# A hybrid decoder step on one core: mask product over 512 columns, small tiles that share areas, a 54th buffer, and a deeper look-ahead in one stretch

## The chip, the cores and the metric

The kernel is one program for one NeuronCore of a Trainium2 chip. The metric is the device time of one execution in microseconds (us). The engines have names here as in the profile: PE (TensorE, matrix products), DVE (VectorE), ACT (ScalarE), POOL (GpSimd) and SP (SyncE, which only issues DMAs). Each engine works through its own list of instructions in order; an instruction that waits holds up all that stand behind it on its engine. PE writes to PSUM, and all the rest works in SBUF or moves between SBUF and device memory by DMA.

## The reference

Two residual layers over 1024 prompt tokens and 8 single new tokens, 2048 channels, all in float32:

```
layer A:  u, gate = x @ w_in_a
          d = trailing mean of u over 2, 4, 8 or 16 tokens (by channel group) - u
          d = (d by group @ w_grp) * scale
          x = LayerNorm(alpha * x + (d * silu(gate)) @ w_out_a)
shared:   k, v = x @ w_kv            # 4 heads of 64; the first 16 dims of k rotated
layer B:  q, gate = x @ w_in_b       # 32 heads of 64; q rotated
          s = q.k / 8 over the last 128 keys; p = exp(s - m) / (sum + exp(sink - m))
          x = LayerNorm(alpha * x + ((p @ v) * silu(gate)) @ w_out_b)
outputs:  x of both token sets, the last 15 pooled rows, the last 128 keys and values
```

In layer B a query at position i of a block of 128 sees the keys 0 to i of its own block and the keys i+1 to 127 of the block before it: 128 keys exactly, split at the diagonal.

## The kernel before, in words

Tokens are worked on in two chunks, c = 0 with 512 and c = 1 with 512 + 8. Channels lie on the partitions. Phases follow each other: "ai" and "ao" (layer A's input and output projection), "bi" and "bo" (layer B's), each for chunk 0 and then chunk 1.

**Products.** The large projections take float32 operands apart: a high part (`cast_to`, ACT, L488) and a low part (`prep_to`, DVE, L503), and three matmuls stand for one (high by high, high by low, low by high; L658 to L660). All but two phase parts use Strassen's scheme: of a pair of output tiles, seven products of 24 matmuls each, whose weight sums are made by DVE (L346 in `first_pair`, L293) and written back for the second chunk. The two plain parts (start of ai0, first half of bi0) use units of 48 matmuls over 512 columns (L686 to L688).

**Look-ahead.** Before each product `begin` runs `load_to(e + a)`, `prep_to(e + d)` and `cast_to(e + b)`: weight loads run `a` products ahead, casts `b`, low parts `d`. The three numbers are 7, 4, 3. From the last pair of queries in bi1 until the 23rd product of bo0 they are 6, 3, 2 (`self.ahead`, set in `queries`). In bi1, `begin` also falls back to 6, 3, 2 when fewer than four buffers are free. This order of the source is kept on PE, DVE and ACT (`in_order`); SP and POOL are ordered by the scheduler of the framework.

**Buffers.** Nearly everything in SBUF lives in one pool (`Mem`) of 53 buffers of 128 x 1040 float32, handed out whole (`full`) or as halves (`half`). `full` takes the buffer given up longest ago. A buffer that was given up by an instruction that has not run yet is no error: whoever writes to it first waits for that instruction. How early side work starts (normalisation, weight sums, activation loads) depends on how many buffers are free.

**Attention** (`attend`, one call for two heads and one chunk, 32 calls). PE's scores (L1760) put 256 keys per block into PSUM: 128 of the block before, 128 of its own. ACT copies the earlier keys to SBUF (L1778), DVE overwrites those at or before the query by the own block's scores where an int32 mask says so (L1782, `copy_predicated`), finds the largest (L1786), ACT takes the exponentials (L1797) and scales by the sums (`norm`, L1810, eight pieces of 128 columns). PE turns the eight 128 x 128 pieces (L1814), ACT copies them (L1823), and DVE makes a second, masked copy (L1824: 1024 columns, times +1, 0 or -1). The values are then two kinds of products (L1848): one half of the keys times all queries as if it belonged wholly to one block, and a correction, the masked copy times the difference of the two blocks' values (`Vd`). Of each 128 queries the correction reads only 64 columns.

Queries come from products; `q_done` swaps rows by four DMAs on SP (`partner`, L1616), and DVE rotates (L1624 twice, then the sum L1731). The first scores of a pair need L1731. The gate's half of layer B's projection, the decode tokens (`decode`) and the output products run between.

**Small tiles.** Constants (`cst`: identity, mask, a matrix of 1/2048, pooling factors), parameters (`prm`), the int32 mask, negated sinks, the carried pooling rows, and three small tiles of the decode tokens (of which two exist twice) have areas of their own.

## Time and profile before

| | us |
|---|---|
| median of 3 runs | 2360.77 (2357.7 to 2366.27) |
| the profiled execution | 2356.38 |
| its span, first to last instruction | 2354.6 |
| PE busy | 2297.3 |
| DVE busy | 1925.9 |
| ACT busy | 1343.1 |

How to read the profile. A row of a timeline has the start (us), the length (us), the engine, the source line, the operation, what it writes and reads, and in brackets how long the engine had been idle and what ended that. A row of the table of waits has the waiting engine, tile and line, what ended the wait, the sum in us, how often, and the longest. In a table of groups the last fields are the busy time, the mean length in ns and the idle time before. A stretch has its bounds and length and then the busy time of each engine with its count of instructions; "PEclk" is the granted share of TensorE's clock. SPq is SP's queue: the length there is the issue.

### The profile page before, as it was taken

Reading aid. Unit: us, or ns where it says so; the run is one execution under the profiler, and the core shown is the slowest. Engines: PE = TensorE matmul, PEld = TensorE weight load, DVE = VectorE, ACT = ScalarE, POOL = GpSimd, SP = SyncE. Lnnn points to the kernel's source line nnn. Section 1 sums busy time; section 2 is a strip of 40 time slices with the busy share of each in tenths; the row PEclk is TensorE's granted clock in tenths of the full one; section 3 lists DMA queues with packets and bytes.
Section 4 is the critical chain, followed back from the end, with each engine's and each line's share of the span. In section 5 each row is a group of like instructions: output and inputs, shape, how many; then the busy total and the mean of one; then the engine's idle time right before and its main releaser. Section 6 shows DMA issues by size and latency. Waiting matters only on the chain. (4 is left out here: it accounts for less than half of the span.)

```text
span 2354.6 us, 49710 instructions
## 1 busy us (share of the span) xinstructions
PE 2297.3 (98%) x19960; PEld 2200.9 (93%) x19960; DVE 1925.9 (82%) x2421; ACT 1343.1 (57%) x2429; POOL 205.5 (9%) x411
## 2 busy tenths in 40 slices
PE   8999999999999999999999899999999999999997
PEld 6899999999999999998788799999999999999997
DVE  8787998776878878978987788887777768888887
ACT  4444446544546547554465566685666678546556
POOL 0111110001000000000111111100000000000000
PEclk9999999999999999999999999999999999999999
DMA  8668789989889989999786766688777768799785
GB/s 293 211 246 303 271 299 346 332 292 319 289 289 339 327 280 333 328 388 327 272 310 220 248 219 239 224 310 270 237 249 245 230 201 305 239 342 372 260 300 199
DMA packets 250919, 665.18 MB, mean 283 GB/s; under 512 B 25632, under 2 KB 106432, under 8 KB 250688
## 3 DMA queue, kind: packets, MB, share of 16 engines
q1 hardware_dynamic: 205216, 496.94, 63.0%
q0 software_dynamic: 45472, 165.07, 18.1%
q8 instruction: 156, 2.56, 0.4%
q14 instruction: 75, 0.61, 0.1%
HBM read 466.81 MB, written 185.59 MB: 277 GB/s over the span
## 5 line engine op out<-in xcount | busy, mean ns | idle before, releaser
L658 PE MATMUL pD<-m,m 128*128 128x260 f32 (+1 forms) x4752 | 1346.0, 283 | 8.1 <-ACT pD L599 4.4
L660 PE MATMUL pD<-m,m 128*128 128x260 f32 (+1 forms) x4752 | 1339.1, 282 | 4.4 <-DVE m L503 4.4
L659 PE MATMUL pD<-m,m 128*128 128x260 f32 (+1 forms) x4752 | 1338.8, 282 | 0.0
L658 PEld LDWEIGHTS pD<-m,m 128*128 128x128 f32 x4752 | 894.5, 188 | 13.7 <-ACT pD L599 5.5
L660 PEld LDWEIGHTS pD<-m,m 128*128 128x128 f32 x4752 | 895.2, 188 | 5.5 <-DVE m L503 5.5
L503 DVE TENSOR_TENSOR m<-m,m 128x1024 fp32r<-128x1024 f32 x674 | 814.5, 1219 | 100.1 <-ACT m L488 60.6
L659 PEld LDWEIGHTS pD<-m,m 128*128 128x128 f32 x4752 | 894.9, 188 | 0.5
L488 ACT CAST m<-m 128x1024 fp32r<-128x1024 f32 x674 | 702.7, 1049 | 324.7 <-DVE m L346 85.1
L686 PE MATMUL pD<-m,m 128*128 128x512 f32 x448 | 179.7, 401 | 8.0 <-ACT m L769 8.0
L687 PE MATMUL pD<-m,m 128*128 128x512 f32 x448 | 177.9, 397 | 1.0 <-DVE m L778 1.0
L688 PE MATMUL pD<-m,m 128*128 128x512 f32 x448 | 177.5, 396 | 0.0
L778 DVE TENSOR_TENSOR m<-m,m 128x1024 fp32r<-128x1024 f32 (+1 forms) x120 | 147.0, 1226 | 6.4 <-ACT m L769 4.7
L769 ACT CAST m<-m 128x1024 fp32r<-128x1024 f32 (+1 forms) x120 | 125.9, 1053 | 17.7 <-PE pD L687 5.2
L631 ACT COPY m<-pD 128x260 f32<-128x260 f32 (+1 forms) x83 | 31.1, 375 | 179.2 <-PE pD L660 179.1
L346 DVE TENSOR_TENSOR m<-m,m 128x1024 f32<-128x1024 f32 x88 | 107.6, 1222 | 12.7 <-DMA m<-in_wib 6.3
L686 PEld LDWEIGHTS pD<-m,m 128*128 128x128 f32 x448 | 85.1, 190 | 28.1 <-ACT m L769 8.0
L687 PEld LDWEIGHTS pD<-m,m 128*128 128x128 f32 x448 | 85.0, 190 | 21.1 <-DVE m L778 2.1
L688 PEld LDWEIGHTS pD<-m,m 128*128 128x128 f32 x448 | 85.0, 190 | 19.7
L1797 ACT ACTIVATE m<-m,sm 128x128 f32<-128x128 f32 x256 | 99.4, 393 | 0.0
L619 DVE TENSOR_TENSOR m<-pD,m 128x260 f32<-128x260 f32 (+1 forms) x86 | 36.5, 424 | 74.4 <-PE pD L660 74.1
L1088 PE MATMUL pD<-m,m 128*128 128x260 f32 (+1 forms) x528 | 91.5, 323 | 0.0
L1088 PEld LDWEIGHTS pD<-m,m 128*128 128x128 f32 x528 | 79.5, 188 | 8.2
(249 smaller groups left out, 2180.9 us busy)
## 6 DMA issues: line engine op xcount, KB each, us to landing
m<-in_wia SPq DMA_DIRECT2D x124, 512.0 KB
m<-in_wib SPq DMA_DIRECT2D x120, 512.0 KB
swia<-m POOLq DMA_DIRECT2D x64, 512.0 KB, 4.8
m<-swia SPq DMA_DIRECT2D x64, 512.0 KB
m<-swoa SPq DMA_DIRECT2D x64, 512.0 KB
swib<-m POOLq DMA_DIRECT2D x64, 512.0 KB, 5.1
m<-swib SPq DMA_DIRECT2D x64, 512.0 KB
m<-swob SPq DMA_DIRECT2D x56, 512.0 KB
```

The lines of the kernel that those rows point to most:

```text
L346: self.nc.vector.tensor_add(s[out].a[:, :1024], s[x].a[:, :1024], s[y].a[:, :1024])
L488: self.nc.scalar.copy(hi.r[:, :1024], self.stream[self.cast].src().a[:, :1024])
L503: self.nc.vector.tensor_sub(lo.r[:, :1024], s.src().a[:, :1024], hi.a[:, :1024])
L658: nc.tensor.matmul(ps[:, :TH], wh[:, s], h, start=new and k == 0, stop=False, skip_group_check=on)
L659: nc.tensor.matmul(ps[:, :TH], wh[:, s], l, start=False, stop=False, skip_group_check=on)
L660: nc.tensor.matmul(ps[:, :TH], wl[:, s], h, start=False, stop=k == 7, skip_group_check=on)
L686: nc.tensor.matmul(ps[:], wh[:, s], h, start=par == 0 and k == 0, stop=False)
L687: nc.tensor.matmul(ps[:], wh[:, s], l, start=False, stop=False)
L688: nc.tensor.matmul(ps[:], wl[:, s], h, start=False, stop=par == 1 and k == 7)
L769: self.nc.scalar.copy(h.r[:, :n], s.a[:, :n])
L778: self.nc.vector.tensor_sub(l.r[:, :n], s.a[:, :n], h.a[:, :n])
L1088: nc.tensor.matmul(ps[:, : cs.stop - cs.start], ws[:, s], d[:, cs], start=f0 and k == 0, stop=l0 and k == 3,)
```

## The change

Four things change together.

- **The keys of a score are stored with the halves swapped for half of the cases.** Each score matmul writes its three blocks of 64 keys in reverse, and for the second head the two row halves are swapped. The mask becomes bytes and has one pattern for each head. After turning, every piece has the two kinds of keys such that the correction needs 64 of its 128 columns, so the masked copy is made over 512 columns and fits a half buffer. That half buffer (`x["wp"]`) is taken at the first `norm`, since two of the eight scaled pieces are written in two halves, one of them there; the scaling is ten instructions.
- **Small tiles share areas.** Carried rows and the decode tiles lie in one tile `area` (the two copies of `qd` and `sgd` become one each); negated sinks overwrite `prm`; the 1/2048 matrix is made on DVE into `jr`, and not loaded; small tiles of the softmax are three for one call instead of four; decode's and the tail's small tiles move into the pool's halves.
- **The pool has 54 buffers.**
- **Look-ahead 7, 4, 3 stays** for the last pair of bi1 and the start of bo0; the fallback in bi1 is at fewer than three free buffers.

```diff
-K_ID, K_MP, K_J, K_RC = 0, 128, 256, 384
-N_CST = 384 + 4 * NST
+K_ID, K_MP, K_RC = 0, 128, 192
+N_CST = 192 + sum(WINDOWS) - 4
-NSLOT = 53
+NSLOT = 54
-        self.mki = one.tile([P, P], I32, name="mki")
+        self.mki = one.tile([P, 2, P], U8, name="mki")
-        self.carry = one.tile([P, NK, NST], F32, name="carry")
-        self.kdec = one.tile([P, 2, NDEC], F32, name="kdec")
-        self.qd = [one.tile([P, NDEC, 8], F32, name=f"qd{i}") for i in range(2)]
-        self.sgd = [one.tile([P, 8, NDEC], F32, name=f"sgd{i}") for i in range(2)]
+        area = one.tile([P, NK * NST], F32, name="area")
+        three = lambda a, b, c: area[:, a : a + b * c].rearrange("p (b c) -> p b c", b=b)
+        self.carry = three(0, NK, NST)
+        self.kdec, self.qd, self.sgd = three(0, 2, NDEC), three(16, NDEC, 8), three(80, 8, NDEC)
...
-        if getattr(self, "ph", "") == "bi1" and len(self.mem.whole()) < 4:
+        if getattr(self, "ph", "") == "bi1" and len(self.mem.whole()) < 3:
...
-                            self.S[u : u + 64, j, b * 256 + u : b * 256 + u + 192],
-                            q[r, b * P + u : b * P + u + 64],
-                            self.kT[t // 8][r, b * P + u : b * P + u + 192], start=True, stop=True,
+                            o.rearrange("p (m k) -> p m k", m=3), q[r, b * P + u : b * P + u + 64],
+                            k.rearrange("p (m k) -> p m k", m=3)[:, ::-1, :], start=True, stop=True,
...
-                s4, self.mki[:, None, None, :].to_broadcast([P, NB, 2, P]), p4[:, :, :, P : 2 * P]
+                s4, self.mki[:, None, :, :].to_broadcast([P, NB, 2, P]), p4[:, :, :, 0:P]
...
-                nc.scalar.activation(x["s3"][:, i, :], x["s3"][:, i, :], AF.Copy, scale=rs[:, i : i + 1])
+                v = x["s3"][:, i, :]
+                parts = [(v, v)]
+                if i in (0, 7):
+                    k1, k0 = v[:, :64], v[:, 64:]
+                    e = x["wp"].a[:, :P]
+                    parts = [(k0, k0), (e[:, 64:], k1)] if i == 0 else [(k1, k1), (e[:, :64], k0)]
+                for out, a in parts:
+                    nc.scalar.activation(out, a, AF.Copy, scale=rs[:, i : i + 1])
...
-            x["w"], x["wp"] = self.mem.full(), self.mem.full()
+            x["w"] = self.mem.full()
             nc.scalar.copy(x["w"].a[:, :1024], PT)
             nc.vector.tensor_mul(
-                x["wp"].a[:, :1024].rearrange("p (i k) -> p i k", k=P),
-                PT.rearrange("p (i k) -> p i k", k=P),
-                cst[:, None, K_MP : K_MP + P].to_broadcast([P, 8, P]),
+                x["wp"].a[:, :512].rearrange("p (b i k) -> p b i k", b=NB, i=2), mixed(slice(0, NB)),
+                cst[:, None, None, K_MP : K_MP + 64].to_broadcast([P, NB, 2, 64]),
             )
...
-                    self.ahead = 6, 3, 2
+                    self.ahead = 7,4,3
```

How this moves instructions, at three places. Buffers have the names m0 to m53 here, with two running numbers behind them.

First SP's queue at the end of bi0's plain part, where weight loads (in_wib) and loads of the next part's activations (th) follow each other. Before:

```order
L287 DMA m33_1722_14842<-in_wib 128x1024
L759 DMA m26_1729_14943<-th0_92 128x4x256
L287 DMA m45_1730_14945<-in_wib 128x1024
L759 DMA m2_1740_15039<-th0_92 128x4x256
L287 DMA m7_1731_14947<-in_wib 128x1024
```

And now:

```order
L287 DMA m17_1720_14839<-in_wib 128x1024
L287 DMA m0_1726_14940<-in_wib 128x1024
L287 DMA m3_1727_14942<-in_wib 128x1024
L759 DMA m37_1736_15033<-th0_86 128x4x256
L759 DMA m22_1737_15035<-th0_86 128x4x256
```

The last two weight loads, which one addition on DVE needs together, stand ahead of the two activation loads.

Second DVE in bi0's Strassen part, at the masked copy of one attention and the rotation for the next pair. Before:

```order
L503 TENSOR_TENSOR m8_1898_16884<-m28_1876_16588,m14_1897_16847 128x1024
L1824 TENSOR_TENSOR m52_1901_16913<-pS_212_12840,cst_76 128x1024
L1624 TENSOR_TENSOR m47_1875_16586<-m47_1875_16586,m29_1533_12852 128x1024
L1624 TENSOR_TENSOR m33_1889_16795<-m33_1889_16795,m29_1533_12852 128x1024
L1731 TENSOR_TENSOR m47_1875_16586<-m47_1875_16586,m33_1889_16795 128x1024
```

And now:

```order
L503 TENSOR_TENSOR m39_1891_16881<-m3_1871_16587,m13_1890_16844 128x1024
L1834 TENSOR_TENSOR m0_1862_16504<-pS_212_12834,cst_76 128x512
L1622 TENSOR_TENSOR m53_1870_16585<-m53_1870_16585,m38_1533_12846 128x1024
L1622 TENSOR_TENSOR m49_1883_16793<-m49_1883_16793,m38_1533_12846 128x1024
L1729 TENSOR_TENSOR m53_1870_16585<-m53_1870_16585,m49_1883_16793 128x1024
```

The place of the masked copy is the same; it has half the columns, and it writes to a buffer with a running number (1862) far older than its neighbours', where before it had just been handed out (1901).

Third DVE at the start of bo0, around the last masked copy; L346 twice is a pair of weight sums. Before:

```order
L1237 SCALAR_TENSOR_TENSOR m35_2549_23919<-m6_2526_23738,m35_2549_23919 128x1024
L1824 TENSOR_TENSOR m5_2604_24409<-pS_212_12840,cst_76 128x1024
L503 TENSOR_TENSOR m2_2605_24412<-m40_2586_24210,m31_2601_24362 128x1024
L346 TENSOR_TENSOR m19_2591_24266<-m40_2586_24210,m19_2591_24266 128x1024
L346 TENSOR_TENSOR m40_2586_24210<-m40_2586_24210,m26_2592_24268 128x1024
```

And now:

```order
L503 TENSOR_TENSOR m33_2574_24358<-m42_2555_24148,m5_2573_24306 128x1024
L346 TENSOR_TENSOR m4_2561_24206<-m42_2555_24148,m4_2561_24206 128x1024
L346 TENSOR_TENSOR m42_2555_24148<-m42_2555_24148,m24_2562_24208 128x1024
L1993 COPY m13_2502_23737<-pS_212_12834 128x128
L1994 TENSOR_REDUCE m13_2502_23737<-m13_2502_23737 128x1
```

The pair of sums, and the low part ahead of it, now stand in front of the decode tokens' work and of the masked copy, one product earlier than before.

More of the change, by code (lines that the diff above doesn't have):

```diff
@@ L11 @@
 F32R = mybir.dt.float32r
-I32 = mybir.dt.int32
+U8 = mybir.dt.uint8
 AF = mybir.ActivationFunctionType
@@ L195, in __init__ @@
         self.cst = one.tile([P, N_CST], F32, name="cst")
-        self.mki = one.tile([P, P], I32, name="mki")
+        self.mki = one.tile([P, 2, P], U8, name="mki")
         self.jr = one.tile([P, P], F32R, name="jr")
-        self.nsink = one.tile([P, NH], F32, name="nsink")
-        self.carry = one.tile([P, NK, NST], F32, name="carry")
-        self.kdec = one.tile([P, 2, NDEC], F32, name="kdec")
-        self.qd = [one.tile([P, NDEC, 8], F32, name=f"qd{i}") for i in range(2)]
-        self.sgd = [one.tile([P, 8, NDEC], F32, name=f"sgd{i}") for i in range(2)]
+        area = one.tile([P, NK * NST], F32, name="area")
+        three = lambda a, b, c: area[:, a : a + b * c].rearrange("p (b c) -> p b c", b=b)
+        self.carry = three(0, NK, NST)
+        self.kdec, self.qd, self.sgd = three(0, 2, NDEC), three(16, NDEC, 8), three(80, 8, NDEC)
         self.flag = one.tile([P, 1], F32, name="flag")
@@ L248, in use_four @@
             for j in range(2):
-                self.nc.vector.memset(S4[64:, j, :, :64], 0.0)
-                self.nc.vector.memset(S4[:64, j, :, 192:], 0.0)
+                a, b = (slice(0, 64), slice(64, P))[:: 1 - 2 * j]
+                self.nc.vector.memset(S4[a, j, :, :64], 0.0)
+                self.nc.vector.memset(S4[b, j, :, 192:], 0.0)
     def psW(self):
@@ L887, in j_sum32 @@
     def j_sum32(self, T, src, out):
-        J = self.cst[:, K_J : K_J + P]
+        J = self.jr[:].bitcast(F32)
         for s in [slice(0, T)] if T <= 512 else [slice(0, T // 2), slice(T // 2, T)]:
@@ L1040, in pool_tile @@
         if c == 0:
-            o = K_RC + g * NST
+            o = K_RC + sum(WINDOWS[:g]) - g
             nc.vector.tensor_mul(
@@ L1049, in pool_tile @@
         if ext is not None:
-            sd = self.small(NDEC, 12)
+            sd = self.small(NDEC, 10)
             nc.vector.tensor_reduce(sd[:], ext[:, i, :, 16 - w : 16], axis=AX.X, op=ALU.add)
@@ L1205, in phase_ai @@
         if T > TP:
-            nc.sync.dma_start(io["npp"], self.carry[:])
+            nc.sync.dma_start(io["npp"], self.carry)
     def phase_out(self, c, res, nxt, last=None):
@@ L1313, in phase_end @@
         TH = T // 2
-        J = self.cst[:, K_J : K_J + P]
+        J = self.jr[:].bitcast(F32)
         A, Bh = slice(0, TH), slice(TH, T)
@@ L1325, in phase_end @@
         A2 = slice(0, 2 * P)
-        four = self.small(NK * 4, 1)
-        f3 = four[:].rearrange("p (k t) -> p k t", k=NK)
+        f3 = self.mem.half().v(NK, 4)
         b2 = lambda x: x[:, None, :].to_broadcast([P, 2, TH])
@@ L1513, in last_four @@
             nc.sync.dma_start(io["y1c"], f3)
-        one = self.small(1, 4)
-        nc.scalar.activation(one[:], self.cst[:, K_J : K_J + 1], AF.Abs_reciprocal_sqrt)
+        nc.scalar.activation(self.small(2, 1)[:, :1], J[:, :1], AF.Abs_reciprocal_sqrt)
         x, y, z = SPLIT
@@ L1735, in b @@
                 nc.vector.tensor_copy(
-                    self.qd[t0 // 8][:, :, o : o + n],
+                    self.qd[:, :, o : o + n],
                     s.v(n, T)[:, :, TP:T].rearrange("p k b -> p b k"),
@@ L1759, in score @@
                         r = slice(64 * j, 64 * j + 64)
+                        z = u if j == 0 else 64 - u
+                        o = self.S[z : z + 64, j, b * 256 + 64 - u : b * 256 + 256 - u]
+                        k = self.kT[t // 8][r, b * P + u : b * P + u + 192]
                         nc.tensor.matmul(
[L1761 to L1763 removed]
+                            o.rearrange("p (m k) -> p m k", m=3), q[r, b * P + u : b * P + u + 64],
+                            k.rearrange("p (m k) -> p m k", m=3)[:, ::-1, :], start=True, stop=True,
                         )
@@ L1777, in select @@
                 b0 = 1
-            nc.scalar.copy(s4[:, b0:], p4[:, b0:, :, 0:P])
+            nc.scalar.copy(s4[:, b0:], p4[:, b0:, :, P : 2 * P])
         def largest():
@@ L1782, in largest @@
             nc.vector.copy_predicated(
-                s4, self.mki[:, None, None, :].to_broadcast([P, NB, 2, P]), p4[:, :, :, P : 2 * P]
+                s4, self.mki[:, None, :, :].to_broadcast([P, NB, 2, P]), p4[:, :, :, 0:P]
             )
-            mx, nm, es, rs = x["sm"] = [self.small(8, 12) for _ in range(4)]
+            mx, nm, es = (self.small(8, 10) for _ in range(3))
+            x["sm"] = mx, nm, es, mx
             nc.vector.tensor_reduce(mx[:], s3, axis=AX.X, op=ALU.max)
             v3 = lambda a: a[:].rearrange("p (b j) -> p b j", j=2)
-            nsk = self.nsink[:, None, 2 * t : 2 * t + 2].to_broadcast([P, NB, 2])
+            nsk = self.prm[:, None, C_SINK + 2 * t : C_SINK + 2 * t + 2].to_broadcast([P, NB, 2])
             nc.vector.scalar_tensor_tensor(v3(nm), v3(mx), -0.125, nsk, op0=ALU.mult, op1=ALU.min)
@@ L1808, in norm, with mixed @@
             rs = x["sm"][3]
+            if n == 0:
+                x["wp"] = self.mem.half()
             for i in range(4 * n, 4 * n + 4):
-                nc.scalar.activation(x["s3"][:, i, :], x["s3"][:, i, :], AF.Copy, scale=rs[:, i : i + 1])
+                v = x["s3"][:, i, :]
[6 more added lines that the diff above has]
+                    nc.scalar.activation(out, a, AF.Copy, scale=rs[:, i : i + 1])
         def turn():
             for i in range(8):
-                nc.tensor.transpose(
-                    PT[:, i * P : (i + 1) * P], x["sc"][:, i * P : (i + 1) * P], cst[:, K_ID : K_ID + P]
-                )
+                a = x["sc"][:, i * P + 64 : (i + 1) * P + 64] if i < 7 else x["wp"].a[:, :P]
+                nc.tensor.transpose(PT[:, i * P : (i + 1) * P], a, cst[:, K_ID : K_ID + P])
             x["s"].free()
+        def mixed(b):
+            return PT.rearrange("p (b i k) -> p b i k", b=NB, i=4)[:, b, 0:4:3, :]
         def keep():
-            x["w"], x["wp"] = self.mem.full(), self.mem.full()
+            x["w"] = self.mem.full()
             nc.scalar.copy(x["w"].a[:, :1024], PT)
             nc.vector.tensor_mul(
-                x["wp"].a[:, :1024].rearrange("p (i k) -> p i k", k=P),
-                PT.rearrange("p (i k) -> p i k", k=P),
-                cst[:, None, K_MP : K_MP + P].to_broadcast([P, 8, P]),
+                x["wp"].a[:, :512].rearrange("p (b i k) -> p b i k", b=NB, i=2), mixed(slice(0, NB)),
+                cst[:, None, None, K_MP : K_MP + 64].to_broadcast([P, NB, 2, 64]),
             )
@@ L1842, in values @@
                         o = x["o"][b // 2]
-                        V, p = (self.Vd[b], x["wp"].a) if step else (self.V[b + 1 - k], x["w"].a)
-                        c0, c1 = (64 * k, 64 * k + 64) if step else (0, P)
+                        V = self.Vd[b] if step else self.V[b + 1 - k]
                         for j in range(2):
                             vs = slice((2 * (t // 8) + j) * HD, (2 * (t // 8) + j + 1) * HD)
-                            m = (2 * b + j) * P
+                            i = (2 * b + j - k) % 8
+                            out = o[64 * j : 64 * j + 64, n * P : (n + 1) * P].rearrange("p (h q) -> p h q", h=2)
+                            if step:
+                                out, p = out[:, k, :], x["wp"].a[r, i * 64 : i * 64 + 64]
+                            else:
+                                p = x["w"].a[r, i * P : i * P + P].rearrange("p (h q) -> p h q", h=2)
+                                if j:
+                                    p = p[:, ::-1, :]
                             ins = nc.tensor.matmul(
-                                o[64 * j : 64 * j + 64, n * P + c0 : n * P + c1], V[r, vs], p[r, m + c0 : m + c1],
+                                out, V[r, vs], p,
                                 start=part == 0 and n == 0 and step == 0, stop=part == 1 and step == 1,
@@ L1913, in rest @@
             if T > TP:
-                d = self.sgd[t0 // 8][:, t0 % 8 : t0 % 8 + n, :]
+                d = self.sgd[:, t0 % 8 : t0 % 8 + n, :]
                 self.at(1, lambda: nc.scalar.copy(d, s.v(n, T)[:, :, TP:T]))
@@ L1956, in decode @@
         st, s, pd, a = (W.a[:, i * P : (i + 1) * P] for i in range(4))
-        mx, es, rs = (self.small(1, 4)[:] for _ in range(3))
+        mx, es, rs = (W.a[:, 4 * P + i : 4 * P + i + 1] for i in range(3))
         sk = self.prm[:, C_SDEC + pr : C_SDEC + pr + 1]
@@ L1964, in s0 @@
                     nc.tensor.matmul(
-                        self.S[:, j, 8 * b : 8 * b + 8], dk[r, b, :], self.qd[pr][r, b, :], start=True, stop=True
+                        self.S[:, j, 8 * b : 8 * b + 8], dk[r, b, :], self.qd[r, b, :], start=True, stop=True
                     )
@@ L2011, in s9 @@
         def s9():
-            a3 = self.sgd[pr][:]
+            a3 = self.sgd
             nc.vector.scalar_tensor_tensor(
@@ L2127, in start @@
         self.at(13, lambda: setattr(self, "x0", None))
-        self.at(9, lambda: nc.scalar.copy(self.jr[:], self.cst[:, K_J : K_J + P]))
-        nc.vector.tensor_scalar(
-            self.nsink[:], self.prm[:, C_SINK : C_SINK + NH], -1.0, None, op0=ALU.mult
-        )
+        ident = self.cst[:, K_ID : K_ID + P]
+        self.at(9, lambda: nc.vector.tensor_scalar(self.jr[:], ident, 0.0, 1.0 / D, op0=ALU.mult, op1=ALU.add))
+        sink = self.prm[:, C_SINK : C_SINK + NH]
+        nc.vector.tensor_scalar(sink, sink, -1.0, None, op0=ALU.mult)
     def run(self):
@@ L2272, in _consts @@
     cst[:, K_ID : K_ID + P] = np.eye(P, dtype=f)
-    cst[:64, K_MP : K_MP + P] = i[:64, None] > i[None, :]
-    cst[64:, K_MP : K_MP + P] = -1.0 * (i[64:, None] <= i[None, :])
-    cst[:, K_J : K_J + P] = 1.0 / D
+    h = i[:64]
+    cst[:64, K_MP : K_MP + 64] = h[:, None] > h[None, :]
+    cst[64:, K_MP : K_MP + 64] = -1.0 * (h[:, None] <= h[None, :])
     for g, w in enumerate(WINDOWS):
-        cst[:, K_RC + g * NST : K_RC + (g + 1) * NST] = w / np.minimum(w, np.arange(NST) + 1.0)
-    return cst, (i[None, :] <= i[:, None]).astype(np.int32)
+        o = K_RC + sum(WINDOWS[:g]) - g
+        cst[:, o : o + w - 1] = w / (np.arange(w - 1) + 1.0)
+    k = (i + 64) % P
+    return cst, np.stack([k[None, :] <= q[:, None] for q in (i, k)], axis=1).astype(np.uint8)
 def kernel(**inputs):
```

## The prediction

> **What bounds the kernel now.** I read the busy times first, then who waits for whom on TensorE (PE), then the stretches around the longest of these waits.

> ```profile
> span 2354.6 us, 49710 instructions
> PE 2297.3 (98%) x19960; PEld 2200.9 (93%) x19960; DVE 1925.9 (82%) x2421; ACT 1343.1 (57%) x2429; POOL 205.5 (9%) x411
> ```

> PE is busy for 98% of the span, and the change takes no product away and adds none. So it can gain only where PE stands still. The table of stretches tells how much that is between the start (20 us) and the tail (2325 us), where the change does little (length, busy time of PE, weight loads, DVE, ACT and POOL, granted clock, DMA share, GB/s):

> ```profile
> 20.00:1326.00 1306.00, 1299.43 (x9872) 1228.11 (x9873) 1077.51 (x1366) 661.77 (x1036) 128.33 (x246) 1.00 0.85 298
> 1326.00:1342.00 16.00, 7.65 (x61) 5.41 (x63) 10.66 (x11) 7.21 (x22) 2.24 (x5) 0.68 0.96 282
> 1342.00:2325.00 983.00, 963.80 (x9907) 946.55 (x9896) 806.71 (x1000) 644.70 (x1324) 73.42 (x152) 1.00 0.78 264
> ```

> Idle are 6.6, 8.4 and 19.2 us, 34 us together: all there is to win, beside a fall of the clock, of which the middle row tells (0.68). PE's waits in that stretch, by what ended them (sum, times, longest):

> ```profile
> PE pS L1760 <- DVE m L1731: 8.4, 8, 1.5
> PE pO L1848 <- ACT m L1823: 7.8, 1, 7.8
> PE pD L660 <- DVE m L503: 4.4, 5, 1.4
> PE pD L658 <- ACT pD L599: 4.4, 5, 1.9
> PE pD L658 <- DVE m L619: 3.7, 4, 1.4
> PE pS L1848 <- DVE m L1824: 1.5, 3, 0.7
> PE pO L1848 <- DVE m L1824: 0.6, 1, 0.6
> ```

> So: scores (L1760) wait for the rotated queries (L1731), once the values (L1848) wait 7.8 us for the copy of the turned weights (L1823), and products wait for low parts (L503) or for a PSUM tile to be cleared (L599, L619).

> **The change, part by part.** *The 7.8 us wait.* The order of time on DVE, ACT and PE around it, and SP's queue before it:

> ```profile
> 1321.97 1.22 DVE L503 TENSOR_TENSOR m<-m,m 128x1024 fp32r<-128x1024 f32 x1
> 1328.94 1.22 DVE L346 TENSOR_TENSOR m<-m,m 128x1024 f32<-128x1024 f32 x1 [5.75 <-DMA m<-in_wib]
> 1330.20 1.04 ACT L488 CAST m<-m 128x1024 fp32r<-128x1024 f32 x1 [9.02 <-DVE m L346]
> 1333.73 1.00 ACT L1823 COPY m<-pS 128x1024 f32<-128x1024 f32 x1
> 1334.79 0.48 PE L1848 MATMUL pO<-m,m 64*64 64x128 f32 x2 [7.79 <-ACT m L1823]
> ...
> 1299.80 0.33 SPq L287 DMA_DIRECT2D m<-in_wib  x1
> 1311.58 0.38 SPq L759 DMA_DIRECT2D m<-th  x1
> 1312.06 0.45 SPq L287 DMA_DIRECT2D m<-in_wib  x1
> 1320.25 0.38 SPq L759 DMA_DIRECT2D m<-th  x1
> 1320.73 0.99 SPq L287 DMA_DIRECT2D m<-in_wib  x1
> ```

> A weight load is issued at 1320.73, because in SP's in-order queue an activation load stands ahead of it that gets a buffer only at 1320.25. DVE's addition L346 waits 5.75 us for it, ACT's cast waits behind that, the copy L1823 behind the cast, and PE behind the copy. In the changed order the two loads that this addition needs stand directly behind each other, ahead of both activation loads, and by their buffer numbers both buffers are given up within the product that now frees the one issued at 1312.06. So the second goes out at about 1312.5 instead of 1320.7 and, at the 8.2 us that it took from issue to L346 (1328.94 - 1320.73), lands before 1321. DVE's idle 5.75 us go; L346 follows L503 at 1323.2, and PE starts the values 5.85 us later (1334.79 - 1328.94), at 1329.0 against 1326.98, when it was ready: 2.0 us of the wait stay. **-5.7** (0 if the load lands no earlier, -7.8 if DVE is ahead too).

> *The clock.* The wait costs more than itself:

> ```profile
> 1331.00:1336.00 5.00, 0.71 (x8) 0.31 (x8) 2.67 (x4) 5.00 (x19) 0.64 (x2) 0.50 0.90 282
> 1340.00:1342.00 2.00, 2.00 (x19) 1.38 (x21) 1.93 (x4) 0.18 (x1) 0.53 (x1) 0.85 0.84 301
> ```

> The granted clock is 0.50 here and comes back at 1340.6 (2.00 us at a mean of 0.85 are 0.6 at half and 1.4 at full clock). PE worked from 1334.8 on, so 5.8 us at half clock, of which half is lost. The waits of up to 1.9 us elsewhere left the clock at 1.00 (rows of the long stretches), so a rest of 2.0 us should too. **-2.9** (or 0). [...]

> *Scores.* In two of these waits the chain on DVE is product, rotation, sum; later pairs wait for the swapped rows:

> ```profile
> 1477.70 1.23 DVE L1824 TENSOR_TENSOR m<-pS,cst 128x1024 f32<-128x1024 f32 x1 [2.48 <-PE pD L659]
> 1478.84 2.35 DVE L1624 TENSOR_TENSOR m<-m,m 128x1024 f32<-128x1024 f32 x2
> 1481.23 1.22 DVE L1731 TENSOR_TENSOR m<-m,m 128x1024 f32<-128x1024 f32 x1
> 1482.51 0.56 PE L1760 MATMUL pS<-m,m 64*64 64x192 f32 x8 [1.15 <-DVE m L1731]
> ...
> 1771.01 2.40 DVE L1624 TENSOR_TENSOR m<-m,m 128x1040 f32<-128x1040 f32 x2 [1.65 <-DMA m<-m]
> 1774.74 0.56 PE L1760 MATMUL pS<-m,m 64*64 64x192 f32 x8 [1.48 <-DVE m L1731]
> ...
> L1824 DVE TENSOR_TENSOR m<-pS,cst 128x1024 f32<-128x1024 f32 x32 | 39.2, 1225 | 57.2 <-ACT m L1823 46.5 <-PE pD L659 9.0 <-ACT m L1810 1.8
> L436 DVE TENSOR_TENSOR m<-m 128x512 f32<-128x512 f32 x56 | 38.3, 683 | 0.0
> L1105 DVE SCALAR_TENSOR_TENSOR m<-pD,prm,m 128x512 f32<-128x512 f32 x16 | 11.8, 747 | 8.2 <-PE pD L1088 8.2
> L1810 ACT ACTIVATE m<-m,sm 128x128 f32<-128x128 f32 x256 | 82.3, 399 | 6.1 <-DVE sm L1805 6.1
> L1782 DVE COPY_PREDICATED m<-mki,pS 128x1024 f32<-128x1024 int32 x32 | 42.2, 1320 | 0.0
> ```

> The product waits for a whole buffer that PE gives up at L659, then takes 1.23 us. Now its half buffer is held since ACT's scaling, so that wait is gone at both places of this kind, and 512 columns take 0.68 (SBUF) to 0.75 (PSUM, three operands): I take 0.7, 0.5 less, 16 us of DVE over 32. Together over 1.5 us earlier: the 1.15 us wait goes. In the later pairs the swap's four copies stood behind a weight load that waited for a buffer; in the new order three such sets are ahead of it, about 2 us earlier (an estimate from how much later in the product that buffer is given up). Of the eight waits five should go, at the mean 8.4 / 8 = 1.05: **-5.2** (0 to -8.4). Values that wait for the product itself (1.5 and 0.6 us): **-1.5** (0 to -2.1).

> *Look-ahead.* Two of the waits for L503 follow a double L346 where the tables were 6, 3, 2:

> ```profile
> 2032.70 2.48 DVE L346 TENSOR_TENSOR m<-m,m 128x1024 f32<-128x1024 f32 x2
> 2038.10 0.39 PE L660 MATMUL pD<-m,m 128*128 128x256 f32 x1 [1.14 <-DVE m L503]
> 2061.85 0.39 PE L660 MATMUL pD<-m,m 128*128 128x256 f32 x1 [1.35 <-DVE m L503]
> ```

> With low parts three products ahead, a burst of 2.48 us is met by one product more (24 matmuls, about 2.9 us). **-2.5** (0 to -2.5).

> *The buffer itself.* One example of a cast that waited for one:

> ```profile
> 355.14 1.05 ACT L488 CAST m<-m 128x1024 fp32r<-128x1024 f32 x1 [6.87 <-DVE m L624]
> 361.04 0.39 PE L658 MATMUL pD<-m,m 128*128 128x256 f32 x1 [1.95 <-ACT pD L599]
> ```

> In the new order that cast's buffer was given up long before, so this one cast of 1.05 us leaves the row of ACT work that L599 stands behind; the others still wait for DVE's data: **-1.0** (0 to -1.9).

> *What is added.* The scaling is ten pieces instead of eight, 64 more ACT instructions. The nearest row is a piece of 128 columns, 399 ns alone; by that the bound is 26 us, and nothing the other, as two halves have the same columns. I take the middle, 13 us: ACT idles 43%, and turning comes products later, so zero on the path; without that cover it would be 0.4 per attention. [...] The byte mask has no row: 1.32 us each if nothing changes, double at worst (42 us of DVE over 32, against 18% idle there); I take no change. Score and value matmuls keep count and columns; no row shows reversed key blocks, and I take the same time. The smaller constants land before their use, as now. Shared small tiles make one new wait: ACT's write of gates for the second half after the first half's store, three products (some 8 us) behind its issue, so nothing.

> Last, the deeper look-ahead takes up to three buffers where the pool has one more. Counting in both orders the casts, sums and low parts whose buffer is given up only within the same product: 214 before, 171 now, but at the end of bi1 and the start of bo0 (about 100 us) 18 after 12. Priced at the mean of PE's waits in the table above without the long one ((30.8 - 7.8) / 26 = 0.9 us), six more cost **+5** (0 to +10).

> Sum: -5.7 - 2.9 - 5.2 - 1.5 - 2.5 - 1.0 + 5 = -13.8. The profiled execution took 2356.4 us (span 2354.6 and 1.8 around it); that gives 2342.6. It ran 4.4 us below the median of 2360.8, so against the median I say **2347 us**.

> **The rivals.** *Only the long wait goes.* Score waits come back at the next limit, since the swapped rows landed late even when issued early (the 1.65 us behind a DMA), and the other gains pay for the new buffer waits: -5.7, 2355. For it: 8 waits of one kind rarely share one cause. Against: the product's own wait of 2.48 us is longer than the stall.
> *The load is issued earlier but lands no earlier*, because DMA is at 0.9 to 1.0 of its engines there. The change then doesn't do what it says at its main place: -5.2 - 1.5 - 2.5 - 1.0 + 5 = -5.2 or less, 2355 to 2360. Against: at 1312 the queue had been empty for 11 us.
> *Starved look-ahead, slower.* From the last pair of bi1 to product 23 of bo0, 37 products, each begins with a cast and a low part whose buffers are freed only by the product before; ACT then stands in front of the PSUM copies L599 and L605 that PE needs. At the mean of 1.14 and 1.35 us a product, 20 such products cost 25 us against the other gains of 16.3: +9, 2370. It decides from 14 products on. For it: 18 tight buffers instead of 12. Against: 18 are not 37, and loads still land in time.

> **How the numbers follow.** Chances: forecast 0.60 (its own range 2340 to 2353), only the long wait 0.24, no earlier landing 0.10, starved 0.06. The range for 8 in 10 is 2338 to 2360: below, the sum without the +5; above, the second and third rival and no change. About 0.5% (12 us) is what a measurement of this kernel can tell from none: under 2349 lies some seven eighths of the forecast's share, 0.52; slower than 2372.6 is the worse half of the last rival, 0.04; within, 0.44.

> **What would show it.** In the new profile: values after L346 wait under 3.4 us at about 1327, and no stretch near 1340 has a clock under 1.00; PE's waits for the sum of the rotation fall from 8 to about 3; the product shows near 700 ns and no wait for L659; no wait for L503 over 1 us near 2036 and 2060; PE's idle between 20 and 2325 us falls from 34 to about 23. Wrong if the idle stays at 34, if PE waits for ACT's L599 or L605 many times between 1980 and 2090, or if the matmul rows of L1760 and L1848 grow.

## The result, and the profile after

| | before | after |
|---|---|---|
| median of 4 runs, us | 2359.23 (2357.18 to 2366.27) | 2331.84 (2330.99 to 2332.49) |
| the profiled execution, us | 2356.38 | 2332.49 |
| span, us | 2354.6 | 2330.7 |

The ratio is 0.9883, with a 95% interval of 0.9866 to 0.9899: 27 us less, where 14 were forecast. In the later comparisons the median of before was 2357.0 to 2358.3, so about 25 us is the better figure; the two spans differ by 23.9. Medians here and below are of executions in the fast state: one slow execution of after (4177.76 us, among the four of after_again) and one of before (4541.84) are left out.

The head of the page of after:

```profile
span 2330.7 us, 49775 instructions
PE 2293.2 (98%) x19960; PEld 2199.7 (94%) x19960; DVE 1908.7 (82%) x2422; ACT 1350.4 (58%) x2492; POOL 205.7 (9%) x411
```

Where the time went is told by three stretches of equal bounds, first of before, then of after (bounds, length, busy time and count of PE, weight loads, DVE, ACT, POOL, granted clock, DMA share, GB/s):

```profile
20.00:1080.00 1060.00, 1055.17 (x8322) 1029.66 (x8323) 875.15 (x1104) 537.79 (x772) 93.01 (x175) 1.00 0.86 305
1080.00:1345.00 265.00, 254.91 (x1642) 206.36 (x1642) 215.98 (x281) 134.18 (x291) 38.65 (x78) 0.98 0.78 271
1345.00:2100.00 755.00, 739.61 (x8042) 724.54 (x8041) 607.42 (x777) 505.46 (x1128) 59.71 (x129) 1.00 0.76 252
```

```profile
20.00:1080.00 1060.00, 1055.47 (x8322) 1030.07 (x8323) 875.56 (x1105) 535.79 (x771) 92.73 (x175) 1.00 0.87 305
1080.00:1345.00 265.00, 262.29 (x1736) 214.50 (x1735) 221.10 (x290) 143.62 (x318) 39.89 (x81) 0.99 0.78 277
1345.00:2100.00 755.00, 749.62 (x8132) 736.25 (x8131) 603.91 (x798) 515.88 (x1180) 60.71 (x131) 1.00 0.78 260
```

In the first 1060 us both run the same 8322 matmuls, although the look-ahead there uses the pool too. The gain begins where attention begins: 94 matmuls more in the second stretch, 90 in the third. By the times at which equal products start, after is level with before at 1075 us (within 0.1), 9.2 us ahead at 1336, 19.1 ahead near 1970 and 23.7 near 2135.

PE's waits in after, from 20 us to the tail, which now begins at 2301 (sum, times, longest):

```profile
PE pD L658 <- DVE m L619: 3.9, 4, 1.3
PE pD L660 <- DVE m L503: 3.1, 2, 2.6
PE pO L1863 <- ACT m L1833: 1.8, 1, 1.8
PE pS L1761 <- DVE m L1729: 1.4, 2, 0.8
PE pD L658 <- ACT pD L599: 1.1, 2, 0.6
PE pS L1863 <- DVE m L1834: 0.8, 2, 0.5
...
PE pO L1863 <- DVE m L1834: 0.3, 1, 0.3
```

All rows of this answer together are 14.8 us, against 34.4 before. (L1761 are the scores, L1729 the sum of the rotation, L1863 the values, L1833 the copy and L1834 the mask product; they were L1760, L1731, L1848, L1823 and L1824.) The place of the long wait, in order of time:

```profile
1303.22 7.22 SPq L287 DMA_DIRECT2D m<-in_wib  x3
1310.56 8.15 SPq L759 DMA_DIRECT2D m<-th  x2
1320.80 1.22 DVE L346 TENSOR_TENSOR m<-m,m 128x1024 f32<-128x1024 f32 x1
1325.60 1.00 ACT L1833 COPY m<-pS 128x1024 f32<-128x1024 f32 x1
1326.65 0.33 PE L1863 MATMUL pO<-m,m 64*64 64x128 f32 x2 [1.82 <-ACT m L1833]
```

The weight loads stand in one row ahead of the activation loads; the addition runs at 1320.8 without a wait; PE waits 1.82 us where it waited 7.79.

### The profile page after: what moved, and what is told of

Read it like the earlier page. It is cut to its first block, busy times and chain, and to the rows that moved or that the text cites. A ratio compares the mean times of both kernels' runs of the same rounds, so it can differ in the third digit from the quotient of the medians.

```text
span 2330.7 us, 49775 instructions
## 1 busy us (share of the span) xinstructions
PE 2293.2 (98%) x19960; PEld 2199.7 (94%) x19960; DVE 1908.7 (82%) x2422; ACT 1350.4 (58%) x2492; POOL 205.7 (9%) x411
## 3 DMA queue, kind: packets, MB, share of 16 engines
q8 instruction: 156, 2.56, 0.4%
## 5 line engine op out<-in xcount | busy, mean ns | idle before, releaser
L658 PE MATMUL pD<-m,m 128*128 128x260 f32 (+1 forms) x4752 | 1346.2, 283 | 5.5 <-DVE m L619 3.9
L660 PE MATMUL pD<-m,m 128*128 128x260 f32 (+1 forms) x4752 | 1339.1, 282 | 3.3 <-DVE m L503 3.1
L659 PE MATMUL pD<-m,m 128*128 128x260 f32 (+1 forms) x4752 | 1339.3, 282 | 0.0
L658 PEld LDWEIGHTS pD<-m,m 128*128 128x128 f32 x4752 | 895.3, 188 | 10.9 <-issue 3.2
L660 PEld LDWEIGHTS pD<-m,m 128*128 128x128 f32 x4752 | 895.8, 189 | 4.0 <-DVE m L503 3.9
L659 PEld LDWEIGHTS pD<-m,m 128*128 128x128 f32 x4752 | 895.6, 188 | 0.5
L503 DVE TENSOR_TENSOR m<-m,m 128x1024 fp32r<-128x1024 f32 x674 | 814.6, 1220 | 72.7 <-ACT m L488 48.3
L488 ACT CAST m<-m 128x1024 fp32r<-128x1024 f32 x674 | 701.5, 1048 | 253.1 <-DVE m L346 77.7
L778 DVE TENSOR_TENSOR m<-m,m 128x1024 fp32r<-128x1024 f32 (+1 forms) x120 | 147.1, 1229 | 9.5 <-ACT m L769 7.9
L346 DVE TENSOR_TENSOR m<-m,m 128x1024 f32<-128x1024 f32 x88 | 107.6, 1223 | 6.9 <-DMA m<-in_wia 4.2
L686 PEld LDWEIGHTS pD<-m,m 128*128 128x128 f32 x448 | 85.0, 190 | 27.9 <-ACT m L769 8.0
L687 PEld LDWEIGHTS pD<-m,m 128*128 128x128 f32 x448 | 85.0, 190 | 20.6 <-DVE m L778 1.9
L688 PEld LDWEIGHTS pD<-m,m 128*128 128x128 f32 x448 | 84.8, 189 | 19.8
L619 DVE TENSOR_TENSOR m<-pD,m 128x260 f32<-128x260 f32 (+1 forms) x86 | 36.5, 425 | 80.9 <-PE pD L660 80.8
L1820 ACT ACTIVATE m<-m,sm 128x128 f32<-128x128 f32 (+1 forms) x320 | 93.9, 372 | 8.9 <-DVE sm L1806 5.5
L1088 PE MATMUL pD<-m,m 128*128 128x260 f32 (+1 forms) x528 | 91.2, 323 | 0.0
```

What stands on the lines that cost most here:

```text
L346: self.nc.vector.tensor_add(s[out].a[:, :1024], s[x].a[:, :1024], s[y].a[:, :1024])
L488: self.nc.scalar.copy(hi.r[:, :1024], self.stream[self.cast].src().a[:, :1024])
L503: self.nc.vector.tensor_sub(lo.r[:, :1024], s.src().a[:, :1024], hi.a[:, :1024])
L658: nc.tensor.matmul(ps[:, :TH], wh[:, s], h, start=new and k == 0, stop=False, skip_group_check=on)
L659: nc.tensor.matmul(ps[:, :TH], wh[:, s], l, start=False, stop=False, skip_group_check=on)
L660: nc.tensor.matmul(ps[:, :TH], wl[:, s], h, start=False, stop=k == 7, skip_group_check=on)
```

## The experiments

Medians in us; before is 2357 to 2358 in each comparison, and each ratio is to the runs of before beside it.

**The buffer alone.** The kernel after with the old mask product and the old look-ahead, and the same with 53 buffers:

```diff
 # buffers_alone: score order, norm, turn, keep and values as before (1024 columns, two whole buffers)
-        if ... len(self.mem.whole()) < 3:
+        if ... len(self.mem.whole()) < 4:
-                    self.ahead = 7,4,3
+                    self.ahead = 6, 3, 2
 # sharing_alone: the same, with the table of carried sums in a small tile of its own, and
-NSLOT = 54
+NSLOT = 53
```

> The kernel after with the whole mask product of before (1024 columns into a whole buffer, scores and weights in the old order) and the old look-ahead (6, 3, 2 and the bound of four free buffers); shared small tiles and 54 buffers stay. Before 2359 us, after 2332. Theory A (each gain has its own cause: mask product frees the score waits, the look-ahead the two waits near 2036 and 2060): only the waits for a buffer can go, 2346 to 2353 us, waits of scores for the rotation stay 6 to 9 with 6 to 9 us. Theory B (the 54th buffer is what counts: casts and loads are all issued earlier): 2334 to 2343, score waits under 4 us. Theory C (the order is reshuffled, gains belong to no part): waits of every kind change in size and place, and this version lies apart from both.

> The kernel before in its mask product, its 53 buffers and its look-ahead, with the small fixed tiles sharing areas, the mask in bytes and the constant 1/D made on the chip: what is left of the change when mask product, buffer and look-ahead are undone. If the buffer is what counts: as before, 2355 to 2359 us, with score waits of 7 to 9 us. If the sharing itself moves the loads: under 2350.

Measured: buffers_alone 2338.1, ratio 0.9920 (0.9904 to 0.9937); sharing_alone 2357.1, ratio 1.000 (0.9986 to 1.0014). The two differ in one buffer (and in where a table of the last phase lies), and it is worth 19 us. PE's waits in sharing_alone and then in buffers_alone (line numbers are one to two off those of before):

```profile
PE pO L1847 <- ACT m L1822: 6.3, 1, 6.3
PE pS L1758 <- DVE m L1729: 6.2, 5, 2.2
PE pD L657 <- ACT pD L598: 5.0, 5, 2.2
```

```profile
PE pO L1846 <- ACT m L1821: 1.9, 1, 1.9
PE pD L657 <- ACT pD L598: 1.7, 3, 0.9
...
PE pS L1757 <- DVE m L1728: 1.2, 3, 0.6
```

What ended DVE's idle time ahead of the mask product, in the view of its line (us, times), again first in sharing_alone and then in buffers_alone, where no other row follows:

```profile
  ACT m L1822: 45.1, 24
  PE pD L658: 9.0, 4
```

```profile
  ACT m L1821: 57.7, 30
```

With the old product, 1.22 us and a whole buffer, the score waits fall from 6.2 to 1.2 us, the long wait from 6.3 to 1.9, and the product no longer waits 9.0 us for a buffer that PE still reads. Theory A is out for the scores: the free buffer is enough. Theory B's range and its sign (score waits under 4 us) both came. Sharing the small tiles changes no time, but its score waits of 6.2 us lie under the 7 to 9 that were expected; whatever moved them gained nothing.

**The mask part alone**, with 53 buffers, and the same with the product issued twice:

```diff
-NSLOT = 54
+NSLOT = 53
-        f3 = self.mem.half().v(NK, 4)
+        four = self.small(NK * 4, 1)
+        f3 = four[:].rearrange("p (k t) -> p k t", k=NK)
 # and the look-ahead 6, 3, 2 with the bound of four; mask_alone_twice also:
-            nc.vector.tensor_mul(
+            for _ in range(2): nc.vector.tensor_mul(
                 x["wp"].a[:, :512]...
```

> The kernel after with 53 buffers, the table of carried sums back in a small tile of its own, and the old look-ahead: of the change the mask product over 512 columns and the shared areas stay. Theory A: score waits fall from 8 to 2 or 3 (8.4 to about 2 us), the product waits for no matmul, 2343 to 2351 us. Theory B: the buffer count is as before, so 2352 to 2360 and score waits above 5 us. Theory C: the long wait near 1327 changes (under 3 or over 9 us) although no buffer is added.

> The kernel with 53 buffers, the half buffer for the masked weights and the old look-ahead, with the mask product issued twice (DVE as busy as before the change). If the half buffer's room made the gain of the mask part alone (2347.8 against 2357): 2346 to 2351. If the shorter product did: 2354 to 2358. After with the product twice was 8.9 us slower than after, so a mixture is likely: 2351 to 2355.

Measured: 2347.8, ratio 0.9962 (0.9948 to 0.9977), and 2358.5, ratio 1.0002 (0.9993 to 1.0011). Alone the mask part gives 9 us, and all of it goes if the product is issued twice. That does not show that the half buffer gave nothing: two short products take 1.38 us where the old one took 1.22, so DVE is 4.5 us busier here than in before (1930.4 against 1925.9). And the long wait has shrunk in both, though no buffer was added and DVE was not relieved in the second, which is what Theory C named as its sign. The row is the same in mask_alone and in mask_alone_twice:

```profile
PE pO L1864 <- ACT m L1834: 1.9, 1, 1.9
```

In its profiled execution mask_alone_twice gains 6 us on before at this place, is still 5.4 us ahead near 1770, and has lost it all by 2032. So the mask part shortens the long wait whatever DVE's load is (likely by its half buffer: in whole_buffer below the wait is back), and DVE's time decides whether that gain is kept; how the 9 us divide between the two stays open. The score waits of mask_alone are 3.3 us (4 times), of mask_alone_twice 4.7 (5 times). The gains do not add: 19 + 9 would be 28, both together (ahead_old, next) give 22.5.

**The look-ahead, and the product on the kernel after.** ahead_old undoes the look-ahead alone; product_twice issues the product twice as above; whole_buffer is ahead_old with `x["wp"] = self.mem.full()` in place of `half()`, so that a whole buffer is held since the scaling.

> The kernel after with the old look-ahead alone (6, 3, 2 from the last pair of the second projection on, and the bound of four free buffers). Theory A: the same as after until about 1990 us; then waits of 1.1 to 1.4 us for low parts come back near 2015 and 2040: 2334 to 2336 us. Rival (the deeper look-ahead starves the pool, as the prediction's +5 had it): no more than 2332, better than after.

> The kernel after with the mask product issued twice into the same half buffer from the same sources: 32 more DVE instructions of about 0.7 us, 22 us, no other buffer and no other place in the order. If its duration frees the score waits: they come back, 6 to 8 waits with 5 to 8 us, 2337 to 2342 us. If it is its buffer, held since the scaling, that does it: score waits stay at 2 or 3 under 3 us, 2332 to 2335 us.

> The kernel with 54 buffers, the short mask product and the old look-ahead, but with a whole buffer for the masked weights, held since the scaling, instead of a half. If free buffers are what counts: worse than with the half (2334.5), and no better than the old product with 54 buffers, 2338 to 2344 us. If the short product counts: 2333 to 2336.

Measured: ahead_old 2334.5, ratio 0.9903 (0.9888 to 0.9918), whose interval overlaps that of after; product_twice 2340.7; whole_buffer 2343.0. In ahead_old two waits of 1.1 and 1.3 us for low parts are back near 2017 and 2040, and after's wait of 1.3 us for L619 near 2033 is gone: the deeper look-ahead neither starves nor gains much. Holding a whole buffer from the scaling on (longer than before did, where it was taken at the product) costs 8.5 us although the product is as short as in ahead_old, and the long wait is back:

```profile
PE pO L1863 <- ACT m L1833: 7.2, 1, 7.2
```

In product_twice, DVE's 22 us more cost 8.9, but not at the scores. Its waits: L619 clears a PSUM tile late, and the values wait for the product itself (2.9 us, against 0.8), while the scores' wait has 0.8 us:

```profile
PE pD L658 <- DVE m L619: 5.0, 4, 2.5
PE pS L1863 <- DVE m L1834: 2.9, 4, 1.3
```

**The long wait by itself.** Before, with one number changed, so that the load comes earlier but no buffer is added:

```diff
-        a, b, d = self.ahead if self.strassen else (5, 4, 3)
+        a, b, d = self.ahead if self.strassen else (5 + (self.c == 0 and self.ph == "bi0"), 4, 3)
```

> The kernel before with one number changed: in the plain part of the second projection weights are loaded six products ahead instead of five, which puts the load that the 7.8 us wait stands for ahead of the activation loads on SP, as in after; mask product, 53 buffers and all else as before. The prediction's sum for this wait and its clock: -5.7 - 2.9, from 2357 to 2348 us, and the waits behind it (score waits of 8 us, two low parts near 2036 and 2060) as before. Rival (what PE wins there is given back later, as with the two moved pieces of work): the wait shrinks, but 2353 to 2358 us, and waits grow between 1340 and 2060.

Measured: 2353.4, ratio 0.9983 (0.9973 to 0.9993): 4 us of the 8.6. In place of the long wait there are 0.4 and 0.8 us, and the clock stays at 1.00 there, but a new one has come before it. A copy of swapped rows (L1616) stands 1.8 us later in SP's queue (1107.83; before 1106.00), behind the earlier loads; DVE's rotation follows it 3.2 us later (1116.12; before 1112.93), and ACT's copy and PE at the end of that row:

```profile
1107.83 2.52 SPq L1616 DMA_DIRECT2D m<-m  x4
...
1116.12 2.36 DVE L1624 TENSOR_TENSOR m<-m,m 128x1024 f32<-128x1024 f32 x2 [4.88 <-DMA m<-m]
...
1135.43 0.98 PE L1685 MATMUL pS<-cst,m 128*128 128x128 f32 x7 [3.07 <-ACT m L2042]
```

Behind the long wait's place, between 1345 and 1400 us, PE has two more waits, where before has none:

```profile
PE pD L658 <- ACT m L1797: 2.1, 1, 2.1
PE pD L658 <- ACT pD L599: 0.9, 1, 0.9
```

**Two waits taken out of after.** One burst of DVE one product later, and ACT's copy ahead of the exponentials; both_moved has the two edits together, and after_again is after once more:

```diff
 # burst_later
-  self.at(n + 4, lambda: self.pool_tile(...))
+  self.at(n + 4 + (c == 0 and g == 3 and i == 2), lambda: self.pool_tile(...))
 # keep_first
-  self.at(at + s1, lambda: self.posts.append(keep))
+  self.at(at + s1, (lambda: self.posts.append(keep)) if self.strassen else keep)
```

> The kernel after with one burst of DVE (the four windowed sums of the last pool tile of the first row block, 3.8 us, near 352 us) one product later, behind the low part that PE waits for; nothing is left out. After has there a wait of 2.56 us and a granted clock of 0.50 from 358.0 to 361.4. Theory (a wait over about 2 us costs itself and half of a 3.4 us stretch at half clock): both go, 2.56 + 1.71 = 4.3 us, 2327.5 us, and no stretch under 1.00 near 358. Rival (the next low part is late by as much, since DVE has the same work to do): the wait moves on by a product, 2331 to 2333.

> The kernel after with ACT's copy of the turned weights, in the plain part of the second projection with a lag of one product, ahead of the exponentials of the next head instead of behind them; nothing is left out. After has there (1324.8 us) a wait of 1.82 us and one of 0.28, and a clock of 0.50 from 1327.4 to 1330.8. Theory: the copy comes at 1323.1 instead of 1325.6, PE does not wait, the clock stays: -1.8 - 0.3 - 1.7, 2328 us. Rival (the clock falls with the change from the plain to the split products, not with the wait): 2329.7 and a stretch of 0.50 still near 1327.

> Both of the two moves together. If they are separate causes, their gains add: 4.3 + 3.8 = 8.1 us, 2323.7 us, and the clock is 1.00 from 20 us to the tail. If the schedule gives one back elsewhere: 2327 to 2330.

> The kernel after once more, beside the others: 2330 to 2333 us if its time is as steady between chips as the earlier runs had it; it is the base for the 1 to 3 us by which the old look-ahead (2334.5) and the two moves (2330.8) differ from it.

Measured: 2332.7, 2333.7, 2330.8; after once more 2331.9 (three executions, 2329.0 to 2335.5). So none of the three can be told from after, and the 8.1 us did not come. In burst_later the wait is 1.8 us, one product on (PE is busy for 1.65 us of the stretch 356.77 to 360.18), and the clock falls there just the same: its mean over the span is 0.996, where after has 0.997. In keep_first the two waits at 1325 us are gone and the clock stays (0.998 over the span); but what follows waits, between 1320 and 1400 us, first in after, then in keep_first:

```profile
PE pO L1863 <- ACT m L1833: 1.8, 1, 1.8
PE pD L658 <- ACT pD L599: 0.6, 1, 0.6
PE pD L658 <- ACT m L1798: 0.5, 1, 0.5
```

```profile
PE pD L658 <- ACT pD L599: 1.9, 2, 1.1
PE pD L658 <- ACT m L1798: 1.7, 1, 1.7
```

By the times at which equal products start, keep_first is ahead of after by 0.8 us before the edit acts, 5.1 at 1336, 2.4 near 1360, 3.8 near 2010, and 0.8 past 2040. Near 2034 it waits 2.4 us for L619, where after waits 1.3, and the clock falls there (0.83 from 2030 to 2040, where after has 1.00). The profiled execution of after_again has that wait of 2.4 and a fall there too (0.996 over the span), so this loss does not need the edit.

**Is DVE's time what is left?**

```diff
 # no_product: the mask product is left out, and the correction reads the unmasked weights
-                            out, p = out[:, k, :], x["wp"].a[r, i * 64 : i * 64 + 64]
+                            out, p = out[:, k, :], x["w"].a[r, i * P : i * P + 64]
 # product_pool: nc.gpsimd.tensor_mul in place of nc.vector.tensor_mul, from ACT's copy x["w"] in place of PSUM
```

> The kernel after without the mask product: left out are its 32 instructions, and the second step of the values reads the unmasked weights, so what it gives is another result; scores, copies and buffers stay. If DVE's load sets the waits that are left: as much faster as the product issued twice was slower, 2332 - 9 = 2323 us. If what is left stands behind other engines: 2329 to 2332.

> The kernel after with the mask product on POOL (9% busy), which reads ACT's copy of the turned weights and not PSUM; nothing is left out. It takes 22 us and the waits for that copy (66 us) off DVE; the product ends later, as POOL starts when ACT's copy has ended. If DVE's time counts and the values are far enough behind: 2324 to 2329 us. If the values then wait for POOL: over 32 heads at 0.5 to 1 us, 2345 to 2360 us.

> The same with ACT's copy put ahead of the exponentials in the plain part of the second projection, where after waits 1.8 us and loses 1.7 to the clock. If both gains hold: 3 us under the one before it; if they are given back as with the two moves alone: the same within 2 us.

Measured: 2329.5, 2339.2 and 2340.5. Without any product the kernel is 2.4 us faster than after, which lies inside the scatter of after_again, against 9 us slower with two: little or nothing of what DVE saves beyond this point reaches the time. On POOL the product takes twice as long as on DVE (median 1402 ns against 692), and PE waits for it (2.6 us at the scores' tile, 3 times) and for POOL's flag, which stands behind it (2.9 us, 3 times). The copy moved ahead (product_pool_keep) again changes nothing that can be told. The view of the product's line in product_pool:

```profile
L1834 POOL TENSOR_TENSOR m<-m,cst x32: 1278/1402/2408, 1202.0 to 2019.0; 128x512 f32<-128x512 f32 x32
```

## Why the prediction was wrong in size, point by point

| term of the sum | forecast | in the profile of after |
|---|---|---|
| 7.8 us wait | -5.7 | -6.0 (7.79 to 1.82) |
| clock | -2.9 | +0.8 |
| scores | -5.2 | -7.0 (8.4 to 1.4) |
| values behind the product | -1.5 | -1.0 (2.1 to 1.1) |
| look-ahead | -2.5 | -1.2 (two waits gone, L619 at 2033 new) |
| cast at 355 | -1.0 | -0.2 (2.78 to 2.56) |
| added buffer waits | +5 | -4.2 (all other waits, 10.8 to 6.6) |

The rows of waits are those of the two tables of waits, 34.4 and 14.8 us in all, and add to -19.6. PE's busy time, in which the clock's +0.8 lies, fell by 4.1 (told under the offset below). Together that is 23.7 of the 23.9 us between the spans.

**The failed step is the +5.** I counted where a buffer is given up late (214 places before, 171 now, but 18 after 12 in one region), and priced only the region in which the count rose. The 43 places fewer were worth nothing in my sum beyond one cast. The runs show the opposite weight: 54 in place of 53 buffers gives 19 us with the old product and 13 with the new one (2347.8 to 2334.5), and the deeper look-ahead, the cause that I gave for the six more, costs nothing that can be measured. In the profile of after, waits that I had no term for went with it: 1.3 us of values behind L614, most of L599's (4.4 to 1.1, of which 1.95 at 359.1 belongs to the cast), 1 us of L619 at 2157. What is shown is that this one buffer more is worth 13 to 19 us; no run has 52 or 55 buffers, and none separates its room from the changed order that comes with it. load_early, which changes an order alone, gave 4.

**The 7.8 us wait** went as worked out: loads in one row, L346 not waiting, 1.8 us left for the 2.0 forecast. But its price was not the mere order of two loads. With the load earlier and no buffer more, half of it was given back at once (load_early); and it shrinks as well with the buffer alone (1.9) or the mask part alone (1.9), in mask_alone_twice without any gain in time. I read it as one of several signs of a short pool; that reading is argued.

**The clock** term was wrong. I argued from waits of up to 1.9 us that a rest of 2.0 would leave the clock. It fell after 1.82 + 0.28 us, for 3.4 us, and a second time at 358, where the wait of 2.56 us now lies in one piece. The 5.8 us that the prediction took as worked at half clock in before had a wait of 0.6 us in them; PE was busy for 5.26:

```profile
1330.36:1340.60 10.24, 5.26 (x40) 4.06 (x41) 7.87 (x8) 6.87 (x21) 1.71 (x4) 0.50 0.92 289
```

In after it works for 6.8 us at half clock, 1.6 more, of which about half is lost: +0.8. (By the rows of after near 358, matmuls of 256 columns start every 0.21 us at half clock and every 0.12 at full clock.)

**Scores**: near in size, partly by luck. The wait of the product for its buffer was a right link (9.0 us to none) but not the whole: in mask_alone the product waits for no buffer either, and 3.3 us of score waits stay, where buffers_alone has 1.2. And the 0.5 us of shortening that I added to it plays no part there: with the product twice the scores wait 0.8 us. What the shorter product does is to leave DVE time for L619 and for the values, which I had priced at 1.5; product_twice puts it at 8.9 us with all that follows, half-clock time included (6.8 us there, 3.4 in after, at the long wait).

**Cast at 355**: it did move (352.13, from 355.14). Then an activation's low part (L778) went ahead of the burst on DVE, and the low part that PE waits for was 1.2 us later instead:

```profile
347.00 1.23 DVE L778 TENSOR_TENSOR m<-m,m 128x1040 fp32r<-128x1040 f32 x1
...
356.18 1.22 DVE L503 TENSOR_TENSOR m<-m,m 128x1024 fp32r<-128x1024 f32 x1
```

**What I costed at nothing** shows in none of PE's waits. The scaling takes 11.6 us more of ACT (93.9 against 82.3; 13 forecast), the byte mask 1319 ns where it took 1320, the score matmuls 325 where they took 326:

```profile
L1820 ACT ACTIVATE m<-m,sm 128x64 f32<-128x64 f32 x128 | 37.4, 341 | 8.9 <-DVE sm L1806 5.5 <-DMA o<-m 3.4
...
L1761 PE MATMUL pS<-m,m 64*64 64x192 f32 x1024 | 47.9, 325 | 1.4 <-DVE m L1729 1.4
L1782 DVE COPY_PREDICATED m<-mki,pS 128x1024 f32<-128x1024 uint8 x32 | 42.2, 1319 | 0.0
```

**The offset.** I added 4.4 us, by which the profiled execution of before ran under the median of three. More runs put that median at 2357 to 2358, so some 3 of these were scatter. And one term was missing: PE's busy time fell too, by 4.1 us (2297.3 to 2293.2), with the same matmuls and although the clock cost 0.8 more. Fewer waits mean fewer places where a row of pipelined matmuls ends: one lasts 282 ns, and the next starts, by the rows of one line, after some 120, so an end costs some 0.16 us. A first matmul after a wait takes 0.39 us, and the next starts 0.22 behind it (357.45 and 357.67 in after), another 0.10. Before has 44 unbroken rows of matmuls and after 32, so twelve fewer are some 3 us, an estimate from these figures. That this is what PE's busy time lost is argued, and the rest is open.

Of the rivals, none came: the gain was not that of the long wait alone, the load did not land late, and the look-ahead was not starved. Of the signs that were named, the short product (692 ns), its missing wait for L659 and the missing waits for low parts near 2036 and 2060 came. The score waits fell from 8 to 2 (3 were forecast), PE's waits to 14.8 us (23 were forecast), and the clock did fall, against the forecast.

## What to carry to other kernels

When many waits of several kinds (scores, casts, cleared tiles, a late load) share one pool, ask what one more buffer, or one held shorter, does to all of them, before each wait is priced with its own cause. A count of tight places has to be priced where it falls as well as where it rises. A wait that is taken away by itself can be worth less than its length (load_early, keep_first): look for the transfer or the copy that is moved back by it, and for the next wait on the same engine.

## What the runs showed of the hardware

The clock falls sooner than the prediction had it, and by a fixed grid. Rows of after around the wait at 1324.8:

```profile
1327.00:1328.00 1.00, 0.72 (x20) 0.63 (x20) 1.00 (x2) 1.00 (x6) 0.00 (x0) 0.70 1.00 353
1328.00:1329.00 1.00, 1.00 (x17) 0.82 (x10) 1.00 (x2) 0.15 (x2) 0.14 (x1) 0.50 1.12 385
...
1330.00:1331.00 1.00, 1.00 (x4) 0.77 (x3) 1.00 (x2) 0.00 (x0) 0.00 (x0) 0.60 1.04 414
...
354.59:358.01 3.42, 0.86 (x7) 0.66 (x6) 3.35 (x7) 1.66 (x3) 0.00 (x0) 1.00 1.02 407
1323.98:1327.39 3.41, 1.31 (x15) 0.58 (x13) 1.08 (x3) 3.41 (x12) 0.11 (x1) 1.00 0.92 304
```

```profile
357.57:360.98 3.41, 1.52 (x13) 1.31 (x12) 3.41 (x4) 3.38 (x7) 0.00 (x0) 1.00 0.92 286
```

Worked out from the matmul rows of all these traces, for the steps at full clock between 20 and 2310 us: after each of the 26 steps with 1.93 us of rest or more the clock fell; between 1.55 and 1.9 it fell in 8 and not in 13; under that, once (1.01 us). So the rest within a step tells more than the length of a wait: the 1.95 us of before brought no fall, the 1.82 + 0.28 of after did. A fall cost PE some 1.5 us in after: in the step at half clock from 358.01 it starts 16 matmuls of 256 columns, and 29 in each of the two steps behind it. Between 1.55 and 1.9 us of rest these traces do not tell what decides. That a wait of one length brings a fall in one execution and none in another would explain part of the scatter of a few us; no run tested that.
